# A depthwise convolution moved from three engines to 32-column tiles of the tensor engine, in a kernel of two transformer blocks

## The chip, the cores and the metric

The kernel runs on one core of one Trainium2 chip, as one launch, in float32. The metric is the time of one execution on the device in microseconds (us). The engines are called as in the profile: PE is the tensor engine (PEld its weight loads), DVE the vector engine, ACT the scalar engine, POOL is GpSimd, and SP issues most transfers. SPq and POOLq are the queues from which SP and POOL issue.

## The reference

The input x is one sequence of 256 tokens with 1024 channels. The first block has two layers. Layer 0 is a conformer convolution, a layer norm over the residual, and a mixture of 16 experts; layer 1 has attention in the place of the convolution. A second block with attention, a linear recurrence and an MLP follows. The change touches the convolution:

```python
def conformer_conv(x, w_pw1, b_pw1, w_dw, b_dw, g, b, w_pw2, b_pw2):
    h = x @ w_pw1 + b_pw1
    a, gate = jnp.split(h, 2, axis=-1)
    h = a * jax.nn.sigmoid(gate)
    h = lax.conv_general_dilated(
        h, w_dw[:, None, :].astype(h.dtype), window_strides=(1,),
        padding=[(CONV_WIDTH - 1, 0)],
        dimension_numbers=("NWC", "WIO", "NWC"),
        feature_group_count=D_MODEL) + b_dw
    h = jax.nn.silu(layer_norm(h, g, b))
    return h @ w_pw2 + b_pw2
...
        x = layer_norm(ALPHA * x + mix, ln_mix_g[l], ln_mix_b[l])
        ffn = grouped_moe(x, router_w, router_bias, moe_w_gate[l], moe_w_up[l], moe_w_down[l])
```

CONV_WIDTH is 31: each channel's output at a token is the sum of 31 products of that channel's own taps with the 31 latest values of that channel. Channels don't mix, which is what depthwise means.

## The kernel before

Channels lie on partitions and tokens along a row, so the 1024 channels make 8 column tiles `ct` of 128 channels by 256 tokens. A function `conv` (around L475 to L640 of the kernel before) is built as a loop over `n` and issues, for each column tile, three steps.

`glu(ct)` multiplies x with 2 x 128 columns of w_pw1 on PE (L495, 16 matmuls of 128x128 weights by 256 columns). ACT forms the sigmoid `sg` of the gate half (L500), and DVE writes the gated value into `hp[ct]` behind 30 zeros (L501). A tap j of the convolution is then the slice `hp[ct][:, j:j+256]` times one number per partition.

`taps(ct)` sums the 31 slices. The table TAPS says how many taps go to PE and how many to ACT with POOL; DVE has the rest. A tap on PE takes a 128x128 diagonal matrix that ACT forms (L511) and one matmul into the PSUM tile `cvb` (L512). A tap of the next group is a product on ACT (L520) and an addition on POOL (L521). A tap on DVE is one multiply-add (L530, the first two are L528). L532, L533 and L543 add the three sums into `cv[:, ct]`. For tile 0 the mean over its channels (`m0`) is taken by a matmul (L538) and later taken off every tile (L540, L542).

`stats(ct)` squares the tile on ACT (L551) and adds the tile's and the squares' sums over channels into `mean` and `sqs` by two matmuls (L552, L553). After the last tile the layer norm follows: ACT copies the mean (L596, `dm`), DVE computes the variance from `m2` on (L600, then L372 to L384 step by step) and scales the tiles (L607, L608), ACT applies SiLU (L613), and `hT` is cast (L615, L616). PE then multiplies by w_pw2 (L632, tile `pj`). The weights of w_pw2 are split in two parts by `halved(h, k, engine)`: a cast on ACT (L559) and a subtraction on the engine named (L560).

Around these steps stand three more. `distance_rows` forms 16 rows of attention biases (L197, L198); `tables` copies them to 128 rows each in DRAM (L207), from SP's queue. `router` prepares the routers' sums: two products on POOL (L249, L250), two sums on DVE (L252, `rsum`) and a matmul on PE (L254, `rsb`). `load_x` (L182) reads x a second time, since its first copy gave its buffers to the squares.

The order on each engine comes from the order of the calls in this loop; a scheduler may move instructions between engines' steps, except where a block is marked as scheduled by hand (`manual_schedule`, `keep_in_program_order`). Weights come through a ring of 20 buffers of 1 MB or less (`unit`), and SP issues a load only when the ring's next buffer has been released by the PE or ACT work that reads it. `ahead(0, EARLY)` issues the first loads of the experts of layer 0 (L705), which run from 180 us.

Of the kernel before, what the change touches and what calls it, by code (L numbers as in the profile page):

```python
# [21 lines left out]
P = 128  # L22
T = 256
D = 1024
KD = D // P
ALPHA = 4.0 ** 0.25
LN_EPS = 1e-5
# [4 lines left out]
CW = 31  # L32
# [58 lines left out]
class Kernel:  # L91
# [56 lines left out]
    def setup(self):  # L148

        nc, c, a = self.nc, self.consts, self.a  # L150
# [5 lines left out]
        self.cpc = self.c.tile([P, NCC], F32, name="cpc")  # L156
        self.wdw = self.c.tile([P, KD, CW], F32, name="wdw")
        self.load_x(0)
# [198 lines left out]
    def rsqrt_steps(self, pool, out, v, eps, n, scale=1.0, sub=None, tags=None):  # L357
# [3 lines left out]
        if tags:  # L361
            s, t, i = (pool.tile([P, 2] + n, d, name="rs", tag=t, bufs=b) for (t, b), d in zip(tags, (F32, F32, I32)))
# [107 lines left out]
    def conv(self):  # L470
        nc, a = self.nc, self.a
        with self.phase("cv") as c:
# [3 lines left out]
            nc.vector.memset(onesm, 1.0 / D)  # L476
            hp = {}
            cv = c.tile([P, KD, T], F32, name="cv", tag="cv")
# [5 lines left out]
            def glu(ct):  # L484
# [12 lines left out]
                hp[ct] = c.tile([P, T + CW - 1], F32, name="hp", bufs=3)  # L497
                nc.gpsimd.memset(hp[ct][:, :CW - 1], 0.0)
                sg = c.tile([P, T], F32, name="sg", bufs=2)
                nc.scalar.activation(sg, b[:, T:], AF.Sigmoid, bias=self.param("a_b_pw1", 8 + ct))  # L500
                nc.vector.scalar_tensor_tensor(hp[ct][:, CW - 1:], b[:, :T], self.param("a_b_pw1", ct), sg,  # L501
                                               op0=OP.add, op1=OP.mult)

            def taps(ct):

                w = self.wdw[:, ct]
                n_pe, n_pool = TAPS[ct]
                pc = self.bank((P, T), name="cvb", tag="cvb", bufs=2)
                for j in range(n_pe):
                    dg = c.tile([P, P], F32, name="dg", bufs=4)  # L510
                    last[:] = [nc.scalar.mul(dg, self.ident, w[:, j:j + 1])]  # L511
                    nc.tensor.matmul(pc, dg, hp[ct][:, j:j + T], start=j == 0, stop=j == n_pe - 1)  # L512
                pr = c.tile([P, T], F32, name="pacc", bufs=2)
                for n, j in enumerate(range(n_pe, n_pe + n_pool)):
                    tp = pr if n == 0 else c.tile([P, T], F32, name="tp", bufs=4)
                    if n == 0:
                        nc.scalar.activation(tp, hp[ct][:, j:j + T], AF.Identity, scale=w[:, j:j + 1],
                                             bias=self.param("a_b_dw", ct))
                    else:
                        nc.scalar.mul(tp, hp[ct][:, j:j + T], w[:, j:j + 1])  # L520
                        nc.gpsimd.tensor_add(pr, pr, tp)  # L521
                j0 = n_pe + n_pool
                c2 = c.tile([P, T], F32, name="c2", bufs=2)
                accs = (c2, cv[:, ct])
                for n, j in enumerate(range(j0, CW)):
                    dst = accs[n % 2]
                    if n < 2:
                        nc.vector.tensor_scalar(dst, hp[ct][:, j:j + T], w[:, j:j + 1], None, op0=OP.mult)  # L528
                    else:
                        nc.vector.scalar_tensor_tensor(dst, hp[ct][:, j:j + T], w[:, j:j + 1], dst,  # L530
                                                       op0=OP.mult, op1=OP.add)
                nc.vector.tensor_add(c2, c2, pc)  # L532
                nc.vector.tensor_add(cv[:, ct], cv[:, ct], c2)  # L533
                if ct == 0:

                    nc.vector.tensor_add(cv[:, 0], cv[:, 0], pr)
                    mb = self.bank((P, T), name="m0b", tag="mean", bufs=1)
                    nc.tensor.matmul(mb, onesm, cv[:, 0], start=True, stop=True)  # L538
                    nc.scalar.mul(m0, mb, float(KD))
                    nc.vector.tensor_sub(cv[:, 0], cv[:, 0], m0)  # L540
                else:
                    nc.gpsimd.tensor_sub(pr, pr, m0)  # L542
                    nc.vector.tensor_add(cv[:, ct], cv[:, ct], pr)  # L543

            def stats(ct):
                if ct == 0:
                    part["mean"] = self.bank((P, T), name="mean", tag="mean", bufs=1)
                if ct % 2 == 0:
                    part["sq"] = self.consts.tile([P, 2, T], F32, name="sq", tag="x", bufs=4)
                sq = part["sq"][:, ct % 2]  # L550
# [4 lines left out]
            raw, w2, last, late = {}, {}, [], self.tc.keep_in_program_order  # L555

# [9 lines left out]
            nc.sync.dma_start(self.wdw, a["taps"].rearrange("p (c j) -> p c j", c=KD))  # L566
            for n in range(1, KD + 3):
                if n < KD:
                    glu(n)
                if n == 1:  # L570
                    rows = self.distance_rows()
                    nc.sync.dma_start(self.second, a["second"])
                if n == 2:
                    self.router(onesm)
                if 0 <= n - 3:
                    stats(n - 3)
                if 0 <= n - 1 < KD:
                    taps(n - 1)
                if n == KD:
                    for h in range(2):  # L580
                        for k in range(2):
                            raw[h, k] = self.rows(a["a_w_pw2"][0][k * 512:k * 512 + 512, h * 512:h * 512 + 512], "r")
                    self.ahead(0, EARLY)
                    self.tables(rows)
                    with self.tc.issue_after(last[0].ins):
                        halved(0, 0, nc.gpsimd)
            self.fresh()
            for t in range(2):
                self.load_x(t)
            mean = part["mean"]  # L590
            dm, rstd, m2 = (c.tile([P, T], F32, name=n, tag=g, bufs=2)
                            for n, g in (("dm", "c2"), ("rstd", "c2"), ("m2", "sg")))
            hT = c.tile([P, KD, T], F32R, name="hT", tag="xT"), self.unit([KD, T], F32R, kind="h")
            rs = [slice(t * P, (t + 1) * P) for t in range(2)]
            for r in rs:
                late(nc.scalar.copy(dm[:, r], mean[:, r]))  # L596
            halved(0, 1, nc.gpsimd)
            with self.tc.manual_schedule(engines={nc.vector.engine}):
                for r in rs:
                    nc.vector.tensor_mul(m2[:, r], dm[:, r], dm[:, r])  # L600
                for _ in zip(*[self.rsqrt_steps(c, rstd[:, r], sqs[:, r], LN_EPS, P, sub=m2[:, r],
                                                     tags=[("tp", 4), ("tp", 4), ("pacc", 2)]) for r in rs]):
                    pass
# [5 lines left out]
            for r in rs:  # L609
                for k in range(0, KD, 2):  # L610
# [1139 lines left out]
def laid_out(v):  # L1750
# [6 lines left out]
    conv = [v[n].reshape(-1, P).T for n in CONV]  # L1757
    taps = v["a_w_dw"][0].reshape(CW, KD, P).transpose(2, 1, 0).reshape(P, KD * CW)
    j = np.arange(4)
# [76 lines left out]
```

## Time and profile before

| what | value |
|---|---|
| median of 3 runs | 1253.8 us (1251.08 to 1253.81) |
| profiled execution, its own time | 1252.51 us |
| its span from first to last instruction | 1250.9 us |
| mean granted clock of PE, share of full speed | 0.965 |
| load and transposes of x | 0 to 9 us |
| convolution | 9 to 127 us |
| its layer norm up to the first matmul with w_pw2 | 127 to 140 us |
| product with w_pw2, layer norm, routing | 140 to 180 us |
| experts of layer 0 | 180 to 398 us |
| all that follows | 398 to 1250.9 us |

The stages are read from the timeline by the first and the last instruction of their lines. Times inside the program are in microseconds from the start of the span.

### The profile page before, as it was taken

How to read it: one execution, taken by the hardware profiler on the slowest of the kernel's cores; microseconds unless marked ns; L12 is line 12 of the kernel's file. 1: busy time of each engine (PE TensorE's matmuls, PEld its weight loads, DVE VectorE, ACT ScalarE, POOL GpSimd, SP SyncE). 2: the span in 40 equal slices, each digit the busy share in tenths (PEclk: the TensorE clock that was granted, in tenths of full speed). 3: DMA queues.
4: the chain of work that ended last, by engine and by line, in shares of the span. 5: the costliest groups of instructions: out<-in, count | busy, mean ns of one | idle time of the engine just before them, and what ended most of it. 6: DMA issues, size and time to landing. Idle time of an engine off the chain costs nothing. (4 is left out here: it accounts for less than half of the span.)

```text
span 1250.9 us, 15597 instructions
## 1 busy us (share of the span) xinstructions
PE 1151.4 (92%) x5764; PEld 781.7 (62%) x5764; DVE 665.3 (53%) x1309; ACT 510.0 (41%) x947; POOL 260.4 (21%) x198
## 2 busy tenths in 40 slices
PE   7974789999998898989999997999989999999998
PEld 6763664443443787754344433777867877888887
DVE  5999752111102797642111105779887755755555
ACT  3444532121112474432111113667645654554443
POOL 3676100000000342100000002113733134122211
PEclk9887889999999899989999998999999999999999
DMA  9954379999999937489999997454444445565662
GB/s 308 399 99 67 120 271 357 373 409 409 409 409 371 324 135 282 159 311 379 367 409 409 409 404 242 145 171 143 140 156 133 137 160 168 169 189 183 200 192 78
DMA packets 137760, 318.83 MB, mean 255 GB/s; under 512 B 8587, under 2 KB 60332, under 8 KB 137676
## 3 DMA queue, kind: packets, MB, share of 16 engines
q1 hardware_dynamic: 135980, 313.15, 70.3%
q0 software_dynamic: 1408, 4.44, 1.1%
q8 instruction: 49, 0.80, 0.3%
q14 instruction: 35, 0.29, 0.1%
q10 hardware_dynamic: 288, 0.16, 0.0%
HBM read 313.86 MB, written 4.19 MB: 254 GB/s over the span
## 5 line engine op out<-in xcount | busy, mean ns | idle before, releaser
L77 POOL TENSOR_TENSOR w<-w 128x1024 fp32r<-128x1024 f32 (+1 forms) x46 | 112.0, 2436 | 741.7 <-ACT w L76 728.3
L824 PE MATMUL gu<-w,xg 128*64 128x512 f32 x1024 | 227.4, 595 | 0.0
L77 DVE TENSOR_TENSOR w<-w 128x1024 fp32r<-128x1024 f32 (+1 forms) x132 | 173.4, 1318 | 78.3 <-ACT w L76 76.1
L76 ACT CAST w<-w 128x1024 fp32r<-128x1024 f32 (+1 forms) x178 | 182.2, 1043 | 80.1 <-PE pr L322 45.5
L824 PEld LDWEIGHTS gu<-w,xg 128*64 128x64 f32 x1024 | 71.6, 137 | 134.5 <-issue 131.8
L829 DVE TENSOR_TENSOR hh<-hh,gu 128x256 f32<-128x256 f32 x32 | 13.5, 421 | 189.9 <-ACT hh L828 189.9
L322 PE MATMUL pr<-w,hT 128*128 128x512 f32 (+1 forms) x432 | 101.6, 390 | 2.8 <-DVE w L77 2.6
L863 PE MATMUL y<-w,hT 128*64 128x512 f32 x448 | 98.8, 593 | 1.7 <-DVE xg L796 1.7
L322 PE MATMUL wk<-w,mr 128*128 128x512 f32 x384 | 91.9, 395 | 0.0
L322 PEld LDWEIGHTS pr<-w,hT 128*128 128x128 f32 x432 | 78.5, 188 | 20.2 <-DVE w L77 3.0
L312 PE MATMUL pr<-mT,w 128*128 128x512 f32 x256 | 89.9, 394 | 0.0
L828 ACT ACTIVATE hh<-gu 128x256 f32<-128x256 f32 x32 | 12.3, 384 | 186.2 <-PE gu L824 186.1
L312 PE MATMUL pr<-hT,w 128*128 128x512 f32 x208 | 77.7, 414 | 5.4 <-DVE cs L337 3.6
L322 PEld LDWEIGHTS wk<-w,mr 128*128 128x128 f32 x384 | 72.1, 188 | 16.8
L854 DVE SCALAR_TENSOR_TENSOR yl<-y,slotgate,yh 128x512 fp32r<-128x512 f32 x32 | 24.0, 751 | 99.9 <-ACT yh L853 99.0
L863 PEld LDWEIGHTS y<-w,hT 128*64 128x64 f32 x448 | 31.7, 137 | 63.4 <-issue 60.2
L309 PE MATMUL pr<-mT,w 128*128 128x256 f32 x256 | 66.3, 280 | 0.1
L521 POOL TENSOR_TENSOR pacc<-pacc,tp 128x256 f32<-128x256 f32 x71 | 60.0, 845 | 28.6 <-ACT tp L520 23.9
L495 PE MATMUL pw<-xT,w 128*128 128x256 f32 x256 | 61.0, 400 | 1.2 <-DMA w<-in_a_w_pw_dram 1.2
L853 ACT ACTIVATE yh<-y,slotgate 128x512 fp32r<-128x512 f32 x32 | 22.0, 687 | 97.6 <-PE y L863 83.4
L309 PE MATMUL pr<-hT,w 128*128 128x256 f32 x208 | 56.4, 289 | 2.2 <-DVE w L77 2.2
L495 PEld LDWEIGHTS pw<-xT,w 128*128 128x128 f32 x256 | 51.9, 203 | 9.5 <-DVE xT L293 1.4
(428 smaller groups left out, 1983.7 us busy)
## 6 DMA issues: line engine op xcount, KB each, us to landing
w<-in_moe_w_gate_dram SPq DMA_DIRECT2D x128, 512.0 KB, 10.2
w<-in_moe_w_up_dram SPq DMA_DIRECT2D x128, 512.0 KB, 10.2
w<-in_moe_w_down_dram SPq DMA_DIRECT2D x56, 1024.0 KB, 12.7
w<-in_w_in_dram SPq DMA_DIRECT2D x29, 1024.0 KB, 5.2
w<-in_w_mlp_up_dram SPq DMA_DIRECT2D x16, 1024.0 KB, 5.7
w<-in_w_mlp_down_dram SPq DMA_DIRECT2D x16, 1024.0 KB, 5.0
w<-in_a_w_pw_dram SPq DMA_DIRECT2D x10, 1024.0 KB, 11.5
w<-in_moe_w_down_dram SPq DMA_DIRECT2D x16, 512.0 KB, 13.5
```

The costliest lines, as they stand in the source:

```text
L76: late(nc.scalar.copy(t[:, 0], src))
L77: late((nc.gpsimd if self.splits == 2 or self.splits % 4 == 3 else nc.vector).tensor_sub(t[:, 1], src, t[:, 0].bitcast(F32)))
L309: nc.tensor.matmul(out[:, T:], w[k][1][:, s], x[k][:, 0], start=False, stop=False)
L312: nc.tensor.matmul(out, w[k][0][:, s], x[k].rearrange("p i t -> p (i t)"), start=k == 0, stop=k == kd - 1)
L322: nc.tensor.matmul(out, x[k0 + k][:, xi, r], wi[:, cols], start=bool(start and k + i == 0), stop=bool(stop and k == n - 1 and i == 2))
L495: nc.tensor.matmul(b[:, s * T:(s + 1) * T], wts[s][:, k, ct % 2 * P:ct % 2 * P + P], xT[:, k], start=k == 0, stop=k == KD - 1)
L521: nc.gpsimd.tensor_add(pr, pr, tp)
L824: nc.tensor.matmul(b[h * 64:h * 64 + 64, :].rearrange("p (j n) -> p j n", j=2), xg[g, kk // 2][:, k, i * CAP:(i + 1) * CAP], w[:, :, k, h ...
L829: nc.vector.tensor_mul(hs[e], hs[e], b[:, 256:])
L853: late(nc.scalar.mul(yh, y, gs[p]))
L854: late(nc.vector.scalar_tensor_tensor(yl, y, gs[p], yh.bitcast(F32), op0=OP.mult, op1=OP.subtract))
L863: nc.tensor.matmul(y[d][i * 64:i * 64 + 64, :], hT[:, i, j % 2, j // 2 * 64:j // 2 * 64 + 64], w[2 * (j // 2) + i][:, j % 2, d * 512:d * 5 ...
```

## The change

All 31 taps, filled up with one tap of zero to 32, go to PE as matmuls over 4 taps and 32 channels at once. From `hp[ct]` a tile `xs[ct]` is made with 4 groups q: partitions 32j to 32j+31 of group q hold the 32 channels of that group, shifted by j tokens. That takes 16 copies of 32 partitions by 284 columns per column tile, 8 on DVE (L516 of the changed kernel) and 8 on ACT (L514). The weights of one matmul are 128 rows by 32 columns, four diagonals of 32x32 on top of each other, and POOL forms all 32 of a column tile by one product of 128x1024 (L523). A column tile then takes 32 matmuls of 32 columns of weights by 256 columns, 8 for each of the 4 groups; a group writes its own 32 partitions of `cvb` (L531). ACT's and POOL's products and sums (L520, L521), DVE's chain (L528, L530) and ACT's diagonals (L511) are gone. One DVE instruction adds bias and mean into `cv` (L545).

The subtractions of `halved` go from POOL to DVE, three of them ahead of the layer norm. The squares have their own buffers, and x is loaded a second time early, among the first loads of the experts (L183). The 16 bias rows go to DRAM and are copied to 128 rows each from POOL's queue (L206, L209). `router` comes three tiles later, and the order of the loads and the first index of the ring (FIRST) change.

```diff
-FIRST = 11
+FIRST = 7
...
-TAPS = [[2, 11], [2, 6], [2, 11], [3, 11], [1, 12], [2, 11], [5, 11], [10, 6]]
+
+TQ, TB = 4, 8
...
-        self.biases = []
+        self.biases, once = [], self.dram.tile([16, 384], F32, name="rows")
+        nc.gpsimd.dma_start(once, rows)
         for i in range(2):
             d = self.dram.tile([8, P, 384], F32, name=f"bias{i}")
-            nc.sync.dma_start(d, rows[8 * i:8 * i + 8, None, :].to_broadcast([8, P, 384]))
+            nc.gpsimd.dma_start(d, once[8 * i:8 * i + 8, None, :].to_broadcast([8, P, 384]))
...
+                n = T + TQ * (TB - 1)
+                xs[ct] = c.tile([P, 4, n], F32, name="xs", bufs=2)
+                for q in range(4):
+                    for j in range(TQ):
+                        dst, src = xs[ct][32 * j:32 * j + 32, q], hp[ct][32 * q:32 * q + 32, j:j + n]
+                        if (q + j) % 2:
+                            nc.scalar.copy(dst, src)
+                        else:
+                            nc.vector.tensor_copy(dst, src)
+
+            def diagonals(ct):
+
+                u = self.unit([2, 4 * TB, 32], kind="S")
+                for i in range(2):
+                    w = self.wdw[:, (ct + i) * 32:(ct + i) * 32 + 32, None].to_broadcast([P, 32, 32])
+                    nc.gpsimd.tensor_mul(u[:, i], self.wdw[:, None, KD * 32:].to_broadcast([P, 32, 32]), w)
+                    dg[ct + i] = u[:, i].rearrange("p (q b) n -> p q b n", q=4)
...
+                for b in range(TB):
+                    for q in range(4):
+                        nc.tensor.matmul(pc[32 * q:32 * q + 32], dg[ct][:, q, b], xs[ct][:, q, TQ * b:TQ * b + T],
+                                         start=b == 0, stop=b == TB - 1)
...
+                    nc.vector.scalar_tensor_tensor(cv[:, ct], pc, bias, m0, op0=OP.add, op1=OP.subtract)
...
-                    with self.tc.issue_after(last[0].ins):
-                        halved(0, 0, nc.gpsimd)
...
+                    if n == KD - 2:
+                        for h in range(2):
+                            for k in range(2):
+                                raw[h, k] = self.rows(a["a_w_pw2"][0][k * 512:k * 512 + 512, h * 512:h * 512 + 512], "r")
+                        self.fresh()
+                        for t in range(2):
+                            self.load_x(t)
+                        self.ahead(0, EARLY)
...
+                    if n >= KD - 1:
+                        halved(*divmod(n - KD + 1, 2), nc.vector)
...
-            halved(0, 1, nc.gpsimd)
...
-            halved(1, 0, nc.vector)
             halved(1, 1, nc.vector)
```

How the instructions then stand on the engines is shown for three engines; a row is a line of the kernel, an operation, and output from input, and "x16" is a count of equal rows.

On PE, before, between the matmuls of the fourth column tile (`pw_352`) and the sixth (`pw_534`):

```order
L495 MATMUL pw_352<-xT,w 128x256 x6
L254 MATMUL rsb<-rsum,onesm 128x64
L512 MATMUL cvb<-hp,dg 128x256 x2
L495 MATMUL pw_352<-xT,w 128x256 x10
L552 MATMUL mean<-cv,onesm 128x256
L553 MATMUL sqs<-sq,onesm 128x256
L512 MATMUL cvb<-hp,dg 128x256 x2
L495 MATMUL pw_445<-xT,w 128x256 x16
```

The same engine in the changed kernel, from the second column tile (`pw_191`) on:

```order
L498 MATMUL pw_191<-xT,w 128x256 x16
L531 MATMUL cvb<-xs,w 32x256 x32
L498 MATMUL pw_273<-xT,w 128x256 x16
L531 MATMUL cvb<-xs,w 32x256 x32
L541 MATMUL m0b<-cv,onesm 128x256
```

and there from the sixth tile (`pw_527`) to the seventh (`pw_621`):

```order
L498 MATMUL pw_527<-xT,w 128x256 x16
L256 MATMUL rsb<-rsum,onesm 128x64
L531 MATMUL cvb<-xs,w 32x256 x32
L552 MATMUL mean<-cv,onesm 128x256
L553 MATMUL sqs<-sq,onesm 128x256
L498 MATMUL pw_621<-xT,w 128x256 x16
```

The one to ten matmuls with full diagonals become 32 narrow ones in one piece, each group between two column tiles' products with w_pw1, and `rsb` now stands directly behind the products of the sixth tile and ahead of the taps of the fifth.

On DVE of the changed kernel, the stretch that `rsb` waits for (`hp<-pw_527` belongs to the sixth column tile):

```order
L505 SCALAR_TENSOR_TENSOR hp<-pw_527,cpc,sg 128x256
L516 COPY xs<-hp 32x284 x8
L254 TENSOR_REDUCE rsum<-rwg 128x2x16
L254 TENSOR_REDUCE rsum<-rwb 128x2x16
L545 SCALAR_TENSOR_TENSOR cv<-cvb,cpc,m_104 128x256
```

The last rows of DVE ahead of the layer norm in the changed kernel (the second L545 is the last column tile's):

```order
L545 SCALAR_TENSOR_TENSOR cv<-cvb,cpc,m_104 128x256
L560 TENSOR_TENSOR w<-w 128x2048
L545 SCALAR_TENSOR_TENSOR cv<-cvb,cpc,m_104 128x256
L560 TENSOR_TENSOR w<-w 128x2048 x2
L619 TENSOR_TENSOR m_879<-tmp 128x128 x2
```

and before (`m_938` and `m_879` are `m2`):

```order
L530 SCALAR_TENSOR_TENSOR c_858<-hp,wdw,c_858 128x256
L532 TENSOR_TENSOR c_858<-c_858,cvb 128x256
L533 TENSOR_TENSOR cv<-cv,c_858 128x256
L543 TENSOR_TENSOR cv<-cv,pacc 128x256
L600 TENSOR_TENSOR m_938<-dm 128x128 x2
```

The sums for `rsb` stand behind the gated value and the eight copies of the sixth tile, and two subtractions of w_pw2 (L560) stand between the last tile and `m2`, where nothing stood before.

On POOL, before, the first additions:

```order
L175 TENSOR_SCALAR alpha<-first 128x128
L249 TENSOR_TENSOR rwg<-second,first 128x256
L521 TENSOR_TENSOR pacc<-pacc,tp 128x256 x10
L498 MEMSET hp 128x30
L521 TENSOR_TENSOR pacc<-pacc,tp 128x256 x5
```

and in the changed kernel the products that form the diagonals:

```order
L176 TENSOR_SCALAR alpha<-first 128x128
L523 TENSOR_TENSOR w<-wdw 128x1024 x4
L251 TENSOR_TENSOR rwg<-second,first 128x256
L501 MEMSET hp 128x30
L502 MEMSET hp 128x2
L523 TENSOR_TENSOR w<-wdw 128x1024 x3
```

and further on there, the copies of the bias rows:

```order
L206 DMA rows<-rows 16x384
L501 MEMSET hp 128x30
L502 MEMSET hp 128x2
L209 DMA bias_485<-rows 1024x1x384
L209 DMA bias_487<-rows 1024x1x384
L252 TENSOR_TENSOR rwb<-second,first 128x256
```

Four products of 128x1024 stand in one piece at the head of POOL's work, three more behind the first memset that waits for the copies of the first tile, and the second product of `router`, `rwb`, stands behind both copies of the bias rows.

## Rows read from the trace of the kernel before

**Rows 1.** Windows: us, busy of PE, PEld, DVE, ACT, POOL, clock, DMA share, GB/s.

```profile
9.00:127.00 118.00, 86.85 (x354) 72.19 (x355) 108.37 (x179) 54.17 (x128) 71.89 (x86) 0.87 0.75 214
127.00:140.00 13.00, 8.51 (x38) 5.96 (x36) 12.80 (x38) 5.29 (x9) 4.51 (x1) 0.89 0.57 202
240.00:398.00 158.00, 154.47 (x760) 65.84 (x756) 23.72 (x60) 29.06 (x54) 0.00 (x0) 1.00 1.03 404
...
62.00:94.00 32.00, 25.68 (x107) 21.61 (x106) 32.00 (x50) 15.44 (x36) 23.32 (x32) 0.89 0.53 105
```

**Rows 2.** Groups by line in 9 to 127 us: busy us, mean ns, idle before.

```profile
L530 DVE SCALAR_TENSOR_TENSOR c<-hp,wdw,c 128x256 f32<-128x256 f32 x65 | 47.7, 734 | 0.0
```

**Rows 3.** Timeline at the end of the stage: start us, us, instruction, idle before it.

```profile
120.02 4.49 POOL L560 TENSOR_TENSOR w<-w 128x2048 fp32r<-128x2048 f32 x1 [1.55 <-ACT w L559]
120.10 4.70 DVE L533 TENSOR_TENSOR cv<-cv,c 128x256 f32<-128x256 f32 x1
124.90 0.42 DVE L543 TENSOR_TENSOR cv<-cv,pacc 128x256 f32<-128x256 f32 x1
126.94 0.49 DVE L600 TENSOR_TENSOR m<-dm 128x128 f32<-128x128 f32 x2 [1.61 <-ACT dm L596]
128.98 4.83 DVE L381 TENSOR_TENSOR rs<-rs 128x128 f32<-128x128 f32 x2
139.50 0.74 PE L632 MATMUL pj<-w,hT 128*128 128x512 f32 x2 [4.49 <-ACT hT L615]
148.59 2.29 DVE L560 TENSOR_TENSOR w<-w 128x2048 fp32r<-128x2048 f32 x1 [1.38 <-ACT w L559]
```

**Rows 4.** Timeline: the first products with w_pw1, and 512-column matmuls at 131 us.

```profile
8.96 14.05 PE L495 MATMUL pw<-xT,w 128*128 128x256 f32 x64 [1.20 <-DMA w<-in_a_w_pw_dram]
...
131.41 3.60 PE L627 MATMUL pj<-x,alpha 128*128 128x512 f32 x8
```

**Rows 5.** Windows of L824 alone, PE and PEld: matmuls of 64 weight columns by 512.

```profile
197.30:197.36 0.06, 0.03 (x2) 0.04 (x2) 1.00 0.99 410
197.30:204.34 7.04, 7.01 (x32) 2.21 (x32) 1.00 0.85 292
```

**Rows 6.** Timeline of DVE, ACT and POOL near the first and fourth tile.

```profile
14.70 1.28 ACT L511 ACTIVATE dg<-first,wdw 128x128 f32<-128x128 f32 x4 [11.85 <-DMA wdw<-in_taps_dram]
17.23 0.35 DVE L528 TENSOR_SCALAR c<-hp,wdw 128x256 f32<-128x256 f32 x1
17.74 2.09 ACT L520 ACTIVATE tp<-hp,wdw 128x256 f32<-128x256 f32 x5
18.31 8.72 POOL L521 TENSOR_TENSOR pacc<-pacc,tp 128x256 f32<-128x256 f32 x10 [2.48 <-ACT tp L520]
19.43 0.94 DVE L530 SCALAR_TENSOR_TENSOR cv<-hp,wdw,cv 128x256 f32<-128x256 f32 x1
28.43 0.47 DVE L530 SCALAR_TENSOR_TENSOR cv<-hp,wdw,cv 128x256 f32<-128x256 f32 x1
29.22 0.53 DVE L198 COPY rows<-db 16x384 f32<-16x384 f32 x1
42.40 0.57 DVE L252 TENSOR_REDUCE rsum<-rwb 128x32 f32<-128x256 f32 x1
```

**Rows 7.** The page's costliest groups: products of 128x1024 on POOL.

```profile
L77 POOL TENSOR_TENSOR w<-w 128x1024 fp32r<-128x1024 f32 (+1 forms) x46 | 112.0, 2436 | 741.7 <-ACT w L76 728.3
```

**Rows 8.** Windows around a pause of PE, columns as in Rows 1.

```profile
26.80:31.30 4.50, 0.17 (x1) 0.00 (x0) 4.50 (x13) 1.97 (x5) 1.25 (x3) 0.96 1.09 348
31.90:34.30 2.40, 2.40 (x7) 1.93 (x6) 2.40 (x4) 1.07 (x3) 2.20 (x3) 0.50 1.05 377
```

**Rows 9.** POOL's transfers by line, SP's queue on the timeline, and a window.

```profile
L1010 POOL DMA_DIRECT2D bias<-bias x8 | 5.8, 732 | 22.9 <-DVE p L1322 10.4 <-DVE m L1259 10.2 <-DVE sel L1253 2.4
...
58.93 14.06 SPq L207 DMA_DIRECT2D bias<-rows  x2
...
139.50:146.90 7.40, 5.89 (x14) 4.39 (x15) 6.11 (x18) 7.37 (x21) 0.00 (x0) 0.54 0.00 0
```

More of the change, by code (lines that the diff above doesn't have):

```diff
@@ L156, in setup @@
         self.cpc = self.c.tile([P, NCC], F32, name="cpc")
-        self.wdw = self.c.tile([P, KD, CW], F32, name="wdw")
+        self.wdw = self.c.tile([P, KD * 32 + 32], F32, name="wdw")
         self.load_x(0)
@@ L361, in rsqrt_steps @@
         if tags:
-            s, t, i = (pool.tile([P, 2] + n, d, name="rs", tag=t, bufs=b) for (t, b), d in zip(tags, (F32, F32, I32)))
+            s, t, i = tags
+            i = i.bitcast(I32)
             s = s[:, 0], s[:, 1], t[:, 0], t[:, 1]
@@ L496, in glu @@
                                          start=k == 0, stop=k == KD - 1)
-                hp[ct] = c.tile([P, T + CW - 1], F32, name="hp", bufs=3)
+                hp[ct] = c.tile([P, T + TQ * TB], F32, name="hp", bufs=3)
                 nc.gpsimd.memset(hp[ct][:, :CW - 1], 0.0)
+                nc.gpsimd.memset(hp[ct][:, T + CW - 1:], 0.0)
                 sg = c.tile([P, T], F32, name="sg", bufs=2)
                 nc.scalar.activation(sg, b[:, T:], AF.Sigmoid, bias=self.param("a_b_pw1", 8 + ct))
-                nc.vector.scalar_tensor_tensor(hp[ct][:, CW - 1:], b[:, :T], self.param("a_b_pw1", ct), sg,
+                nc.vector.scalar_tensor_tensor(hp[ct][:, CW - 1:T + CW - 1], b[:, :T], self.param("a_b_pw1", ct), sg,
@@ L508, in taps @@
                 pc = self.bank((P, T), name="cvb", tag="cvb", bufs=2)
[L509 to L531, printed above, removed]
@@ L532, in taps @@
-                nc.vector.tensor_add(c2, c2, pc)
-                nc.vector.tensor_add(cv[:, ct], cv[:, ct], c2)
+                for b in range(TB):
+                    for q in range(4):
+                        nc.tensor.matmul(pc[32 * q:32 * q + 32], dg[ct][:, q, b], xs[ct][:, q, TQ * b:TQ * b + T],
+                                         start=b == 0, stop=b == TB - 1)
+                bias = self.param("a_b_dw", ct)
+                if ct:
+                    yield
                 if ct == 0:
-                    nc.vector.tensor_add(cv[:, 0], cv[:, 0], pr)
+                    nc.vector.tensor_scalar(cv[:, 0], pc, bias, None, op0=OP.add)
+                    yield
@@ L547, in stats @@
                     part["mean"] = self.bank((P, T), name="mean", tag="mean", bufs=1)
-                if ct % 2 == 0:
-                    part["sq"] = self.consts.tile([P, 2, T], F32, name="sq", tag="x", bufs=4)
-                sq = part["sq"][:, ct % 2]
+                sq = c.tile([P, T], F32, name="sq")
                 nc.scalar.activation(sq, cv[:, ct], AF.Square)
@@ L553, in stats @@
                 nc.tensor.matmul(sqs, onesm, sq, start=ct == 0, stop=ct == KD - 1)
-            raw, w2, last, late = {}, {}, [], self.tc.keep_in_program_order
+            raw, w2, late = {}, {}, self.tc.keep_in_program_order
             def halved(h, k, eng):
@@ L565, in conv @@
                 glu(0)
[L566 to L584, printed above, removed]
-                    with self.tc.issue_after(last[0].ins):
-                        halved(0, 0, nc.gpsimd)
@@ L587, in conv @@
-            self.fresh()
-            for t in range(2):
-                self.load_x(t)
-            mean = part["mean"]
-            dm, rstd, m2 = (c.tile([P, T], F32, name=n, tag=g, bufs=2)
-                            for n, g in (("dm", "c2"), ("rstd", "c2"), ("m2", "sg")))
+                nc.sync.dma_start(self.wdw, a["taps"])
+                diagonals(0)
+                ends = []
+                for n in range(1, KD + 2):
+                    if n < KD:
+                        glu(n)
+                    if n % 2 and n + 1 < KD:
+                        diagonals(n + 1)
+                    if n == 1:
+                        nc.sync.dma_start(self.second, a["second"])
+                    if n == 3:
+                        rows = self.distance_rows()
+                    if n == 4:
+                        self.tables(rows)
+                    if n == 5:
+                        self.router(onesm)
+                    if n == KD - 2:
[6 more added lines that the diff above has]
+                        self.ahead(0, EARLY)
+                    if n == KD:
+                        stats(n - 3)
+                        stats(n - 2)
+                    if n <= KD:
+                        ends.append(taps(n - 1))
+                        next(ends[-1])
+                    if n > 1:
+                        for end in ends:
+                            next(end, None)
+                        ends.clear()
+                    if n < KD and 0 <= n - 3:
+                        stats(n - 3)
+                    if n == KD + 1:
+                        stats(n - 2)
+                    if n >= KD - 1:
+                        halved(*divmod(n - KD + 1, 2), nc.vector)
@@ L593, in conv @@
+            mean = part["mean"]
+            m2 = c.tile([P, T], F32, name="m2", tag="sg", bufs=2)
+            tmp = [c.tile([P, 4, T], F32, name="tmp", tag="xs", bufs=2) for _ in range(2)]
+            dm, rstd = tmp[0][:, 0], tmp[0][:, 1]
+            steps = [[v.rearrange("p (i n) -> p i n", i=2) for v in vs]
+                     for vs in ((tmp[0][:, 2], tmp[0][:, 3], tmp[1][:, 0]), (tmp[1][:, 1], tmp[1][:, 2], tmp[1][:, 3]))]
             hT = c.tile([P, KD, T], F32R, name="hT", tag="xT"), self.unit([KD, T], F32R, kind="h")
@@ L600, in conv @@
                     nc.vector.tensor_mul(m2[:, r], dm[:, r], dm[:, r])
-                for _ in zip(*[self.rsqrt_steps(c, rstd[:, r], sqs[:, r], LN_EPS, P, sub=m2[:, r],
-                                                     tags=[("tp", 4), ("tp", 4), ("pacc", 2)]) for r in rs]):
+                for _ in zip(*[self.rsqrt_steps(c, rstd[:, r], sqs[:, r], LN_EPS, P, sub=m2[:, r], tags=v)
+                               for r, v in zip(rs, steps)]):
                     pass
@@ L1757, in laid_out @@
     conv = [v[n].reshape(-1, P).T for n in CONV]
-    taps = v["a_w_dw"][0].reshape(CW, KD, P).transpose(2, 1, 0).reshape(P, KD * CW)
+    taps = np.concatenate([v["a_w_dw"][0], np.zeros((TQ * TB - CW, D), f)]).reshape(TB, TQ, KD, 4, 32)
+    taps = taps.transpose(1, 4, 2, 3, 0).reshape(P, KD * 32)
+    taps = np.concatenate([taps, (i[:, None] % 32 == np.arange(32)[None, :]).astype(f)], axis=1)
     j = np.arange(4)
```

6 lines of the change are left out of this document (1 added, 5 removed).

## The prediction

> **What bounds the kernel now.** I read the windows by stage first. In the convolution, 9 to 127 us, PE is busy 86.9 of 118 us at a mean clock of 0.87, DVE 108.4, POOL 71.9 and ACT 54.2; from 62 to 94 us DVE is busy 32.00 of 32.00 us [rows 1]. The groups by line say with what: one of DVE's two chains of taps alone is 65 instructions of 734 ns [rows 2]. DVE's queue sets this stage, and PE waits for it. A tap on DVE costs 0.47 us when POOL rests and 0.94 beside POOL's additions, whose pitch is 8.72/10 = 0.87 us: one DVE instruction gets through per POOL instruction [rows 6]. So POOL's share of the taps is paid for by DVE.
>
> The end of the stage comes next, on the timeline. The last sum stands 4.70 us beside one POOL subtraction of 4.49 us; the last tile is complete at 124.90 + 0.42 = 125.3 us, `m2` starts at 126.94, one step of the root stands 4.83 us (its form takes 0.49 for two elsewhere), and the first product with w_pw2 starts at 139.50 us [rows 3]. From there to the end nothing in the change alters the work, and in the experts' stage PE is busy 154.5 of 158 us [rows 1]. So the question is when that first product starts; I carry its shift to the end one to one. The bound on that is the experts' transfers, which run at 404 GB/s, a share of 1.03 [rows 1]. They start on PE's releases: with the ring full the transfers stand at 0 GB/s from 139.5 to 146.9 us [rows 9], so they shift with PE.
>
> **PE's path after the change.** DVE's 14 us or so per tile go; what is left is 8 copies and two short instructions, some 3.5 us, so PE becomes the bound, and I add up PE's row of work.
>
> A product with w_pw1 is 32 records; 64 take 14.05 us, the last 0.4 of it pipelined, so a record of 256 columns steps by (14.05 - 0.4)/63 = 0.217 us and a tile by 6.93 [rows 4]. Eight tiles make 55.4 us.
>
> The taps are 32 matmuls of two records, 64 records a tile. The trace has no tile of 32 columns. The nearest is L824 with 64: 512-column records of 128 weight columns step by 3.60/8 = 0.45 us [rows 4], but 32 of the 64-wide ones take 7.01 us, 0.219 each, and two of them start within 0.06 us [rows 5]. Two halves of the array therefore ran at once. The ends for 32 columns are four at once, 16 x 0.217 = 3.5 us, and two at once, 32 x 0.217 = 6.9 us; one at a time would be 13.9. I take four, since the halves behave as separate queues and the kernel issues the four groups in turn, with 0.2 us to fill and empty: 3.65 us a tile, 29.2 in all. Weight loads lie beside it (2.21 of 7.04 us [rows 5]).
>
> The Trainium skill, TensorEngine Tiling (Array Packing), sections Theoretical Speedup and Tiling Modes, lists 128x32 as four independent tiles with up to four times the speed, and says that a change of mode drains the engine. By its first half the sum is the one above; sixteen drains aren't priced there, and no run here shows a 32-wide one.
>
> The small ones: `m0b` and the distance rows about 1.1 us, the sums of seven tiles 28 x 0.217 = 6.1, `rsb` and early biases of w_pw2 0.5; 7.7 together. PE starts at 8.96 [rows 4], so without a wait the last taps end at 8.96 + 55.4 + 29.2 + 7.7 = 101.3 us.
>
> **Two waits that the change adds.** First, `rsb` stands on PE behind the sixth tile's products, and its sums stand on DVE behind that tile's gated value and eight copies. In the first tile the gated value was done 1.2 us after PE (from 8.96 + 6.93 = 15.9 to 17.2 [rows 6]). A copy of 284 columns lies between L528, which takes 0.35 and, with the next one overlapping, steps by less, and 0.53 for another copy [rows 6]; I take 0.30, nearest to L528. The two sums take 0.5 each. PE stands 1.2 + 2.4 + 1.0 = 4.6 us (5.5 to 6.4 with the dearer copies), and the fifth tile's taps and all behind them with it. After a pause of 4.5 us PE's granted clock was 0.50, the lower level, to 34.3 us [rows 8]: the 3.0 us from 31.3 on did half their work. I add 1.5 us.
>
> Second, the first tile's copies. The taps land at 14.70 [rows 6], and POOL then has four products of 128x1024 at 2.44 us [rows 7] and a short one, up to 25.1 us without a gap. The gated value is there at 17.2. If a copy gets through only once per POOL instruction, as the additions of taps did [rows 6], three get in by 24.5, and five more end at about 27.0; PE is free at 8.96 + 14.05 = 23.0. PE waits 4.0 us and again loses 1.5 to the clock. The ends are 0, if the copies get through, and 6.3, if none does before 25.1 and each takes 0.53. The second tile's copies are held by the next three products too, but have 11 us of cover under the first taps and the third tile's products. ACT's eight copies at 2.09/5 = 0.42 us [rows 6] take 3.4 us and lie under the 6.9 us of the next products; at the last tile under the seventh's taps and sums.
>
> The Trainium skill, SBUF — State Buffer, section Who interferes with whom, calls the port pair of DVE and GpSimd an exclusive lock for a whole instruction, and exempts DVE instructions with at most one SBUF input outside its two-port modes. The rows of taps agree for two inputs; whether a 32-partition copy is exempt no row says, and that is the fork between my forecast and its best rival.
>
> **The end of the stage.** The last taps end at 101.3 + 4.6 + 1.5 + 4.0 + 1.5 = 112.9; `cv` is complete 0.6 later, 113.5. Then DVE has two subtractions of w_pw2, which cost 2.29 us on DVE with POOL idle [rows 3], so `m2` starts 4.7 us later, 118.2 (before, 1.6 us after the tile; the mean's path lies under them). From `m2` to the first product were 12.56 us; with no POOL subtraction beside the root 4.83 - 0.49 = 4.3 of it go, 8.2 are left: 126.4 us against 139.50. The sum is -13.1 us.
>
> **Edits that I cost at nothing.** The early load of x stands behind a first load of the experts and has one part that waits for the bias rows, near 50 us; the experts' loads queue behind it on SP. Refilling 20 buffers, 10 MB at 404 GB/s [rows 1], takes 25 us, and they are needed from 180 on: 100 us of cover. Without it each microsecond of delay would be paid. The copies of the bias rows leave SP, where the two took 14.06 us to issue [rows 9], for POOL. POOL's transfers of 128 rows took 732 ns each [rows 9]; 2048 rows cost between 1.5 us (per instruction) and 16 x 0.73 = 11.7 us (per row). I take the dearer one: POOL is free at about 65 us, `rwb` behind it by 66, and the sums need it at about 76. Hidden by 10 us.
>
> **Against which time.** The profiled execution took 1252.5 us around a span of 1250.9, 1.3 below the median of 1253.8. 1252.5 - 13.1 = 1239.4, and on the median 1240.7: I say 1241.
>
> **Rivals.**
> (a) Only two narrow tiles run at once: 8 x 3.3 = 26 us more, 1267, slower. Rows 5 show two and no more; for four speaks that the two shared nothing visible. It decides for slower from 3.65 + 13.1/8 = 5.3 us a tile. One at a time would be 8 x 10.2 = 82 more, 1323. 12% and 2%.
> (b) The copies aren't held by POOL's products: 5.5 us better, 1235. 18%.
> (c) The waits are dearer: draining at both ends of the taps, copies at 0.53, late sums, another half-clock stretch: 16 x 0.2 + 1.8 + 1.5 = 6.5 us, 1247. For it speaks that the clock already drops after PE's pauses [rows 8]; against it that PE has fewer pauses. 15%.
> (d) POOL is held until the bias rows have moved. The 3.1 MB at no more than the 105 GB/s of 62 to 94 us [rows 1] take 30 us from 51 on: `rwb` comes at 81, 5 us late, at half that rate 35 us late: 1246 to 1276. Against it: 732 ns per transfer, too short for one that lands within the instruction. 4%.
> (e) The gain is eaten by the experts' transfers, which already run without a gap [rows 1], so that the stage ends where it did: 1253. Against it stands that they wait for PE's releases. 5%.
>
> **The numbers.** My forecast, 1238 to 1244, has 44%. 0.3%, about 3.8 us, is what a measurement of this kernel can tell from no change. Faster are the forecast, (b), (c) and a little of (d): 78%. Within it lies (e) and the top of (c): 7%. Slower are (a) and most of (d): 15%. The range starts at 1230, below (b), since the copies may also cost less, and ends at 1255, above (c) and (e); left out are (a) and the dear half of (d).
>
> **What would show it.** In the profile after: the 64 records of one tile's taps span 3.6 us (6.9 refutes the main term, 13.9 the change); DVE is busy under half of the stage; PE's list of waits shows `rsb` at about 4.6 us behind the sums, and the first taps at about 4 behind a copy; the first eight copies end at 27, with durations near 2.4 us beside L523; `m2` starts 4.7 us behind the last tile; no DVE step of the root stands over 1 us; the first product with w_pw2 starts near 126 us and every later stage is about 13 us earlier. If the product is early and the end is not, (e) holds.

## The result and the profile after

The changed kernel takes 1237.9 us (median of 4 runs, 1237.39 to 1238.38) against 1252.44 us before in the same comparison: a ratio of 0.9881 with a 95% interval of 0.9865 to 0.9897. It is 14.5 us faster; 1241 was forecast, and the measured time lies inside the stated range of 1230 to 1255. The span of the profiled execution falls from 1250.9 to 1236.7 us.

The windows of the changed kernel by stage (us, busy time of PE, PEld, DVE, ACT, POOL, granted clock, DMA share, GB/s) answer to [rows 1]:

```profile
9.00:114.00 105.00, 99.42 (x812) 74.70 (x813) 39.88 (x87) 38.75 (x85) 20.12 (x23) 0.95 0.73 256
114.00:127.00 13.00, 7.52 (x37) 4.89 (x35) 12.75 (x42) 5.94 (x12) 0.00 (x0) 0.95 0.46 163
227.00:385.00 158.00, 154.42 (x758) 65.99 (x756) 24.62 (x63) 30.37 (x55) 0.00 (x0) 1.00 1.03 404
```

PE is now busy 99.4 of 105 us and DVE 39.9: the bound has changed sides. The experts' stage is the one of before, PE busy 154.4 of 158 us at 404 GB/s, only 13 us earlier.

The timeline of the first tiles (start, duration, instruction, idle before) answers to [rows 4] and [rows 6]:

```profile
9.72 15.65 PE L498 MATMUL pw<-xT,w 128*128 128x256 f32 x64 [1.20 <-DMA w<-in_a_w_pw_dram]
...
15.52 7.57 POOL L523 TENSOR_TENSOR w<-wdw 128x1024 f32<-128x1024 f32 x4 [10.24 <-DMA wdw<-in_taps_dram]
...
19.61 5.91 DVE L516 COPY xs<-hp 32x284 f32<-32x284 f32 x8
...
25.31 3.97 PE L531 MATMUL cvb<-xs,w 128*32 128x256 f32 x64
...
29.21 7.17 PE L498 MATMUL pw<-xT,w 128*128 128x256 f32 x32
...
36.31 3.66 PE L531 MATMUL cvb<-xs,w 128*32 128x256 f32 x64
...
37.58 2.49 DVE L516 COPY xs<-hp 32x284 f32<-32x284 f32 x8
```

A tile's 64 narrow records span 3.66 us where nothing disturbs them. The first eight copies take 5.91 us beside POOL's products, the third tile's eight 2.49. Yet the first taps start as soon as PE is free of its first products, which themselves took 15.65 us and not 14.05.

The list of PE's waits from 9 to 130 us, and then the timeline around `rsb` and at the end of the stage, which answers to [rows 3]:

```profile
PE pj L650 <- ACT hT L634: 5.5, 1, 5.5
PE rsb L256 <- DVE rsum L254: 4.9, 1, 4.9
PE pw L498 <- DMA w<-in_a_w_pw_dram: 1.2, 1, 1.2
...
```

```profile
76.23 0.66 PE L256 MATMUL rsb<-rsum,onesm 128*128 128x64 f32 x2 [4.85 <-DVE rsum L254]
76.82 5.82 PE L531 MATMUL cvb<-xs,w 128*32 128x256 f32 x64
...
109.15 3.66 PE L531 MATMUL cvb<-xs,w 128*32 128x256 f32 x64
...
112.88 0.48 DVE L545 SCALAR_TENSOR_TENSOR cv<-cvb,cpc,m 128x256 f32<-128x256 f32 x1 [4.38 <-PE cvb L531]
113.28 4.65 DVE L560 TENSOR_TENSOR w<-w 128x2048 fp32r<-128x2048 f32 x2
...
117.85 0.49 DVE L619 TENSOR_TENSOR m<-tmp 128x128 f32<-128x128 f32 x2
...
125.91 1.22 PE L650 MATMUL pj<-w,hT 128*128 128x512 f32 x2 [5.48 <-ACT hT L634]
```

`rsb` stands 4.85 us for its sums, and the taps behind it take 5.82 us at a mean granted clock of 0.62 (76.8 to 82.7 us). `m2` starts 5.0 us behind the last taps, 4.5 us after the last tile is complete (112.88 + 0.48), and the first product with w_pw2 at 125.91 in the place of 139.50 [rows 3]: 13.6 of the span's 14.2 us are there.

### The profile page after: what moved, and what is told of

It is laid out like the page before. It is cut to its first block, busy times and chain, and to the rows that moved or that the text cites. A ratio compares the mean times of both kernels' runs of the same rounds, so it can differ in the third digit from the quotient of the medians.

```text
span 1236.7 us, 16265 instructions
## 1 busy us (share of the span) xinstructions
PE 1163.2 (94%) x6222; PEld 783.2 (63%) x6222; DVE 593.9 (48%) x1217; ACT 492.9 (40%) x905; POOL 204.9 (17%) x137
## 5 line engine op out<-in xcount | busy, mean ns | idle before, releaser
L498 PE MATMUL pw<-xT,w 128*128 128x256 f32 x256 | 58.2, 387 | 1.2 <-DMA w<-in_a_w_pw_dram 1.2
L314 PEld LDWEIGHTS pr<-mT,w 128*128 128x128 f32 x256 | 46.8, 188 | 9.1
```

What stands on the lines that cost most here:

```text
L314: nc.tensor.matmul(out, w[k][0][:, s], x[k].rearrange("p i t -> p (i t)"), start=k == 0, stop=k == kd - 1)
```

## The experiments

Each run is compared with the kernel before on the same chip; before stood at 1253.0 to 1253.6 us in these comparisons. My theory: PE's row of work, the matmuls in the order of its queue with their waits, up to the first product with w_pw2 sets the time, and its shift reaches the end. The chief rivals: the experts' transfers take back what PE gains (e), POOL's products hold the copies or don't (b), two narrow tiles run at once or four (a).

**The router's sums ahead of the sixth tile** (`router` yields before its matmul):

```diff
+        yield
         o = self.bank((P, 4 * NE), name="rsb", tag="cvb", bufs=2)
...
+                    if n == 5:
+                        sums = self.router(onesm)
+                        next(sums)
                     if n < KD:
                         glu(n)
...
-                        self.router(onesm)
+                        next(sums, None)
```

> The changed kernel with the two router sums on DVE ahead of the sixth tile's gated value and copies, and the router matmul on PE where it was. If PE's row of work up to the first product with w_pw2 sets the time and its shift reaches the end one to one, the wait of 4.85 us and the 2.2 us of half clock behind it go: -7.0 us, 1231 us. If the experts' transfers at 404 GB/s set the end of that stage, PE arrives earlier at the experts and then waits: 1237 to 1239 us, with a wait of PE for a transfer of expert weights that the changed kernel doesn't have.

1230.66 us, ratio 0.9814 (0.9796 to 0.9833). The timeline of PE:

```profile
70.73 0.33 PE L257 MATMUL rsb<-rsum,onesm 128*128 128x64 f32 x2
70.99 3.66 PE L532 MATMUL cvb<-xs,w 128*32 128x256 f32 x64
...
117.93 1.22 PE L654 MATMUL pj<-w,hT 128*128 128x512 f32 x2 [5.47 <-ACT hT L638]
```

The wait is gone, and so is the slow stretch behind it; 7.2 us less in the end. What PE gains reaches the end, and (e) falls.

**Three subtractions of w_pw2 earlier in the loop:**

```diff
-                    if n >= KD - 1:
-                        halved(*divmod(n - KD + 1, 2), nc.vector)
+                    if KD - 2 <= n < KD:
+                        for k in range(KD - n):
+                            halved(n - KD + 2, k, nc.vector)
```

> The changed kernel with three of the subtractions of w_pw2 (and their casts) in the seventh and eighth step of the loop, so that none stands between the last tile and m2. If m2 waits for DVE's queue there, it starts 2.0 to 2.8 us earlier, as soon as ACT has copied the mean, and the whole gets 2 to 3 us shorter: 1235 to 1236 us. If the mean's path through PE and ACT is as late as DVE's queue, nothing moves: 1237 to 1239 us. If the subtractions hold the last tiles' copies instead, PE waits for copies and it gets slower than 1239.

1235.85 us, ratio 0.9859 (0.9832 to 0.9885), 2.1 us less than the changed kernel, though the intervals overlap: the time alone doesn't show the gain. Its timeline does, and it has the first tile without the slow start too:

```profile
9.76 14.05 PE L498 MATMUL pw<-xT,w 128*128 128x256 f32 x64 [1.20 <-DMA w<-in_a_w_pw_dram]
...
18.04 7.21 DVE L516 COPY xs<-hp 32x284 f32<-32x284 f32 x8
...
23.75 5.26 PE L531 MATMUL cvb<-xs,w 128*32 128x256 f32 x64
...
115.43 0.49 DVE L620 TENSOR_TENSOR m<-tmp 128x128 f32<-128x128 f32 x2 [1.72 <-ACT tmp L617]
...
123.50 1.22 PE L651 MATMUL pj<-w,hT 128*128 128x512 f32 x2 [2.72 <-ACT hT L635]
```

`m2` now waits 1.7 us for ACT's copy of the mean and no longer for DVE's queue. From the last taps to the first product with w_pw2 are 10.3 us (113.2 to 123.5) and not 13.1. With the first products at full speed the copies are late: the first taps take 5.26 us, 1.6 more than undisturbed.

**Four groups one after another:**

```diff
-                for b in range(TB):
-                    for q in range(4):
+                for q in range(4):
+                    for b in range(TB):
```

> The changed kernel with the two loops of a tile's taps exchanged: the eight matmuls of one group of 32 channels stand together, then the next group's, instead of the groups in turn. Same number of matmuls, same weights, same results. If only neighbours in PE's queue run at once, a tile's 64 records step by 0.217 us one after another: 13.9 us a tile instead of 3.66, 8 x 10.2 = 82 us more, 1315 to 1325 us. If each narrow tile has a queue of its own that is deep enough for eight matmuls, a tile stays at 3.7 us: 1238 us. Anything between tells how far PE looks ahead.

1301.32 us, in one execution. The timeline of the second tile:

```profile
44.27 11.50 PE L531 MATMUL cvb<-xs,w 128*32 128x256 f32 x64
```

A tile takes 11.50 us, 7.84 more, and eight of them 62.7 of the 63.4 us lost. Narrow tiles run at once only where they are neighbours in PE's queue, with a little overlap at each change of the group: 64 records one after another would be 64 x 0.217 = 13.9 us.

**Two groups in turn, then the other two:**

```diff
-                for b in range(TB):
-                    for q in range(4):
+                for b, q in [(b, q) for h in (0, 2) for b in range(TB) for q in (h, h + 1)]:
+                    if True:
```

> The changed kernel with two groups of a tile in turn, then the other two, in the place of four: the middle between the changed kernel (3.66 us a tile) and the loops exchanged (11.50 us). If records run at once as far as neighbours in the queue belong to different narrow tiles, a pair steps by 0.217 us: 6.9 to 7.1 us a tile, 8 x 3.3 = 26 us more, 1263 to 1266 us. If PE can start a later group ahead by as much as 11.50 us shows (some three records saved at each change of the group), it is a little less, 6.3 to 6.9 us.

1256.5 us, in one execution. The same tile on the timeline:

```profile
37.12 6.27 PE L531 MATMUL cvb<-xs,w 128*32 128x256 f32 x64
```

This is what rival (a) would have been: 2.6 us more a tile, and no faster than before.

**The products that form the diagonals all at the head of POOL's work:**

```diff
-                diagonals(0)
+                for ct in range(0, KD, 2):
+                    diagonals(ct)
...
-                    if n % 2 and n + 1 < KD:
-                        diagonals(n + 1)
```

> The changed kernel with all eight products that form the diagonals (L523) in one piece at the head of POOL's work, instead of four, three and one: the suspected holder of the first tile's copies is doubled. If a copy gets through only once per product, the first eight copies end not near 25.5 us but near 31, six of them at steps of 1.9 us; the first taps end 6 us later and PE loses 1.5 to 3.5 us more to the clock: 1244 to 1248 us. If the copies are free of POOL's products, they take 2.5 us and nothing moves: 1237 to 1239 us.

1245.57 us, ratio 0.9939 (0.9915 to 0.9962), 7.7 us slower than the changed kernel. Its timeline:

```profile
15.38 15.30 POOL L523 TENSOR_TENSOR w<-wdw 128x1024 f32<-128x1024 f32 x8 [10.25 <-DMA wdw<-in_taps_dram]
...
19.65 11.84 DVE L516 COPY xs<-hp 32x284 f32<-32x284 f32 x8
...
30.98 5.23 PE L531 MATMUL cvb<-xs,w 128*32 128x256 f32 x60 [3.26 <-DVE xs L516]
```

Twice the products, and the eight copies take 11.84 us and not 5.91; PE waits for them in the middle of the first taps. POOL's products hold them, about one copy to a product.

**The loads as before** (bias rows from SP's queue behind the first expert loads, then x):

```diff
-        nc.gpsimd.dma_start(once, rows)
...
-            nc.gpsimd.dma_start(d, once[8 * i:8 * i + 8, None, :].to_broadcast([8, P, 384]))
+            nc.sync.dma_start(d, rows[8 * i:8 * i + 8, None, :].to_broadcast([8, P, 384]))
...
-                    if n == 4:
-                        self.tables(rows)
...
-                        self.fresh()
-                        for t in range(2):
-                            self.load_x(t)
                         self.ahead(0, EARLY)
+                        self.tables(rows)
+                        self.fresh()
+                        for t in range(2):
+                            self.load_x(t)
```

> The changed kernel with the loads as before: bias rows copied from SP's queue behind the first expert loads, x loaded a second time behind them. The convolution on narrow tiles stays. If these edits lie under 60 to 100 us of cover, the time stays: 1237 to 1239 us. If the early loads give a part of the 14.5 us (experts' weights earlier, or SP's queue free earlier), it goes back by that part: 1241 us or more, with the experts' stage longer or its first loads late.

1239.29 us, ratio 0.9887 (0.9866 to 0.9907): 1.4 us more than the changed kernel, not told apart from it. But the list of PE's waits has a new row at its head:

```profile
PE pj L643 <- DMA x<-in_x_dram: 10.8, 1, 10.8
```

and the timeline shows what x stood behind:

```profile
59.44 14.85 SPq L208 DMA_DIRECT2D bias<-rows  x2
74.34 51.91 SPq L183 DMA_DIRECT2D x<-in_x_dram  x4
```

PE waits for x until 126.5 us, and the first product with w_pw2 comes at 131.49, 5.6 us later than in the changed kernel. Most of that is given back behind the product: PE spends its stretch at a lower clock on the products with x here (0.62 from 126.6 to 131.4 us), and in the changed kernel on those with w_pw2. The windows of this run and of the changed kernel:

```profile
131.00:171.00 40.00, 34.38 (x177) 27.37 (x176) 18.36 (x67) 13.51 (x23) 0.00 (x0) 0.96 0.69 265
```

```profile
127.00:167.00 40.00, 33.56 (x164) 26.53 (x164) 22.28 (x77) 18.27 (x36) 0.00 (x0) 0.88 0.56 210
```

The experts' first matmuls (`gu`) start only 1.9 us later, at 171.51 and not 169.62. The kernel before had x as late, but not its use. Its timeline:

```profile
77.36 50.94 SPq L182 DMA_DIRECT2D x<-in_x_dram  x4
```

There SP was done with x at 128.3 us, 3.1 us before PE used it at 131.41 [rows 4]; the shorter convolution asks for it earlier.

**Only x as before**, the bias rows on POOL's queue:

```diff
-                        self.fresh()
-                        for t in range(2):
-                            self.load_x(t)
                         self.ahead(0, EARLY)
+                        self.fresh()
+                        for t in range(2):
+                            self.load_x(t)
```

> The changed kernel with the second load of x behind the first loads of the experts, as before, but with the bias rows still copied from POOL's queue: one half of the run with the loads as before, in which PE stood 10.8 us for x until 126.5 us. If x was late there because it stood behind the bias rows in SP's queue, it now lands before 100 us, PE doesn't wait for it, and the time is that of the changed kernel: 1237 to 1239 us. If x is late because it stands behind the experts' loads, PE waits for it again by 5 us or more: 1239 us or above.

1237.61 us, ratio 0.9877 (0.9854 to 0.9901), and no wait for x. Its timeline:

```profile
59.77 7.32 SPq L183 DMA_DIRECT2D x<-in_x_dram  x4
```

So x was late behind the bias rows in SP's queue and not behind the experts. Moving the bias rows to POOL's queue is enough by itself; the early load of x without that was not run.

**Both waits removed**, by the first two edits above together, line for line:

> The changed kernel with the router sums early and three subtractions of w_pw2 early together. If both waits are separate parts of PE's row up to the first product with w_pw2, the gains add: 7.2 + 2.1 = 9.3 us, 1228 to 1229 us. If the second only uncovers the first's wait (or the experts' transfers begin to limit), the sum is less: 1230 to 1231 us, as with the sums alone.

1228.88 us, ratio 0.9802 (0.9781 to 0.9823): 9.0 us less than the changed kernel, near the sum of the two (9.3). Beside the sums alone it is 1.8 us less, and the intervals overlap, so in time alone the second edit's part stays uncertain.

**The same, with PE's rests filled:**

```diff
                 xT = self.transposed(c)
+                self.warm(2, self.bank(name="warm", tag="pw", bufs=4))
                 glu(0)
...
+            self.warm(6, self.bank(name="warm", tag="cvb", bufs=2))
             banks = lambda s: self.bank(s, name="rt", tag="cvb", bufs=2)
```

> The last kernel with matmuls on ones where PE would rest: two behind the transposes of x and six ahead of the first product with w_pw2 (0.43 us each). They compute nothing that is used. If PE's rests are what lowers the granted clock there, the two half-clock stretches (3.4 us at 10 us, 6.8 to 10.2 us at the product with w_pw2) go, worth 1.6 where the first one falls and 3.4 to 5: 1223 to 1226 us. If the clock doesn't follow these rests, the time stays at the last kernel's; if the six stand in the way of the product, it is up to 1 us longer.

1225.4 us, ratio 0.9785 (0.9764 to 0.9806), which overlaps with the last. The windows at the first product with w_pw2, of the kernel without the filling and of this one:

```profile
115.50:122.50 7.00, 5.82 (x13) 4.11 (x14) 5.97 (x17) 6.97 (x20) 0.00 (x0) 0.52 0.00 0
```

```profile
115.10:122.10 7.00, 5.94 (x25) 4.54 (x25) 6.01 (x17) 6.84 (x19) 0.00 (x0) 1.00 0.00 0
```

At a clock of 1.00 and not 0.52, PE does 25 records in seven microseconds and not 13. One profile of each doesn't show that the filling did it, as the next run tells; and whether the two ahead of the first products did anything isn't shown, since these ran in 14.05 us in some kernels without them too.

**And the products on DVE**, so that POOL reads nothing beside the first copies:

```diff
-                    nc.gpsimd.tensor_mul(u[:, i], self.wdw[:, None, KD * 32:].to_broadcast([P, 32, 32]), w)
+                    nc.vector.tensor_mul(u[:, i], self.wdw[:, None, KD * 32:].to_broadcast([P, 32, 32]), w)
```

> The fastest kernel so far (sums early, subtractions early, filling matmuls) with the eight products that form the diagonals on DVE in the place of POOL, so that POOL reads nothing while the first copies run. Three or four of them stand ahead of the copies on DVE, at 1.2 to 1.3 us as DVE's other products of 128x1024. If it is POOL's products that hold the copies, the eight copies take 2.5 us, not 7.2, and end at 23.4, when PE is free: the first taps take 3.7 us, not 5.4, and the time falls by 1.7 us: 1223 to 1224 us. If copies of 32 partitions are slow for another reason beside the first transfers, they stay slow and behind the products too: 1227 to 1230 us.

1225.31 us, ratio 0.977 (0.9751 to 0.9789). Its timeline and a window:

```profile
19.68 2.56 DVE L517 COPY xs<-hp 32x284 f32<-32x284 f32 x8
...
22.63 3.66 PE L532 MATMUL cvb<-xs,w 128*32 128x256 f32 x64
```

```profile
114.20:121.00 6.80, 6.10 (x14) 4.80 (x15) 4.51 (x13) 5.26 (x15) 0.00 (x0) 0.50 0.00 0
```

The copies take 2.56 us and the first taps 3.66: POOL's products were the cause. The 1.7 us expected in the time didn't come. In this profile, taken of the slowest of the five executions (1227.19 us, the fastest 1223.28), the clock stood at 0.50 again from 114 us on, behind the same six filling matmuls. Why they held the clock in one profile and not in the other stays open.

## Why the prediction was right, step by step

**The bound.** Right: DVE's work went from 108 to 40 us of the stage and PE became the row that counts.

**Narrow tiles.** Right: 3.66 us against 3.65, so four at once. Rival (a) is what the kernel does when only two groups stand in turn, at 6.27 us a tile. The Trainium skill, TensorEngine Tiling (Array Packing), section Theoretical Speedup, gives up to four times; the trace agrees with 3.8, from 3.66 us and the estimate of 13.9 for 64 records one after another. The Trainium skill, same page, section Tiling Modes, says that a change of mode drains the engine. Here no drain of more than 0.2 us can be seen: from the third tile's products at 29.21 to the taps at 36.31 are 7.10 us, against 32 x 0.217 = 6.94.

**The wait of `rsb`.** Right, and a little small: 4.85 and 2.2 us against 4.6 and 1.5. Its removal gave 7.2 us.

**The first copies.** The mechanism was right and the size wrong. The step that failed is "PE waits 4.0 us and again loses 1.5 to the clock". A product on POOL took 7.57/4 = 1.9 us here; the 2.44 that I took from [rows 7] is the mean of a group elsewhere in the program. The sum was off by itself too: five copies behind the products at my own 0.30 us end 1.5 us after 24.5, at 26.0 and not 27.0. In the changed kernel's profile the copies ended at 25.5 us, and PE's first products took 1.6 us longer, at about half the clock of the run with the subtractions early, and hid what was left. The windows of the two:

```profile
9.70:13.00 3.30, 3.28 (x8) 2.67 (x9) 0.00 (x0) 0.00 (x0) 0.00 (x0) 0.50 1.19 287
```

```profile
9.70:13.00 3.30, 3.24 (x15) 2.90 (x16) 0.00 (x0) 0.00 (x0) 0.00 (x0) 1.00 1.17 291
```

In the profiles where the products took 14.05 us, POOL formed the diagonals and four groups went in turn, the wait was 1.6 to 1.7 us (5.26 against 3.66 with the subtractions early), and there the clock stayed at 1.00 behind it (23.7 to 29.0 us). The Trainium skill, SBUF — State Buffer, section Who interferes with whom, calls the port pair of DVE and GpSimd an exclusive lock. The runs with eight products on POOL (11.84 us for the eight copies) and with none (2.56) agree, and copies of 32 partitions aren't exempt. Rival (b) was wrong in its cause, and near the truth in its time.

**The end of the stage.** Right: `m2` 4.5 us after the tile is complete (4.7), 8.1 from there to the product (8.2), 125.91 against 126.4.

**The sum.** The last taps were to end at 112.9 and did at 112.8, with errors that cancel, which is luck: 5.2 us less for the copies; 0.8 more for a later start, 1.6 for the slow first products, 0.9 for `rsb`; the remaining 1.8 are steps of 0.1 to 0.2 us between pieces of PE's row, which I hadn't counted. Behind the product another 0.6 us went that I can't place. The measured 1237.9 us is 2.8 below the sum on the median, 1240.7: 1.4 of it is the median before, which is 1252.44 in this comparison and was 1253.8, and 1.4 the gain, 14.5 and not 13.1. So the time lies 0.1 us under the 1238 to 1244 that I gave 44%. The chances for faster, the same and slower are a little off as sums: the rivals' own make about 76, 7 and 17%, not 78, 7 and 15.

**The edits costed at nothing.** For the loads, right in the time, and incomplete: I asked what they cost and not what they prevent. Without them the shorter convolution runs into x, 10.8 us late behind the bias rows. The squares' own buffers and the ring's first index weren't tested by themselves. Rival (d) was far off: POOL issued both copies of the bias rows in 2.19 us, close to the lower bound of 1.5:

```profile
54.23 2.19 POOL L209 DMA_DIRECT2D bias<-rows  x2 [1.73 <-DMA rows<-rows]
60.93 0.61 POOL L252 TENSOR_TENSOR rwb<-second,first 128x256 f32<-128x256 f32 x1 [4.52 <-DVE hp L505]
```

(timeline of the changed kernel: `rwb` waited for a buffer that DVE freed, not for the transfers).

**One to one to the end.** Right: 13.6 us at the product became 14.2 of span, and 9.0 us more reached the end when both waits were removed. Rival (e) is out.

## What to carry to other kernels

When work moves from a bound engine to another, write the new bound's queue down row by row: what it adds to wait for (here 4.9 and 4.5 us behind DVE's queue) is found there before any run, and was worth 9 us more. Narrow matmuls paid here only with neighbours in the queue that belong to different tiles of the array; the order of two loops decided over 63 us. And an edit that is hidden now should also be tried without: it may be what keeps the next wait from showing.

## What the runs showed that I had not expected

The next narrow group overlaps the last one a little: four groups one behind the other took 11.50 us and not 13.9, two pairs 6.27 and not 6.94. That is 0.7 to 0.8 us at each change of the group. In the second tile of that run, which begins at 44.27 us, microseconds in the middle of a group hold 5 to 7 records and those around the three changes (from 46.6, 49.5 and 52.3 us on) 10 or 11.

The first products ran at either clock in profiles of kernels that are equal up to there: 14.05 us (clock 1.00 from 9.7 to 13 us) with the subtractions early, 15.65 in the changed kernel. PE's waits just before them don't tell which: they were 0.99 and 1.20 us in the changed kernel, and 1.27 and 1.21 with the loads as before, where the products took 14.05 us. A single profile's first 25 us therefore don't tell whether the copies cost anything.
